# A decoder layer whose half-steps multiply weights in pairs by seven products: the plain groups in another order, one operand in two pieces, sums made tile by tile

## The chip, the core and the metric

The kernel runs on one core of a Trainium2 chip. Metric: device microseconds of one execution; 2087.26 us is the median of three runs before the change.

## What is computed

One layer on 256 tokens of width 2048: a SwiGLU half-step, a mixer (dilated attention beside gated linear attention), a cross-attention into 256 memory tokens, and a second SwiGLU half-step. The change lies in the half-steps alone:

```
def swiglu(h, w_gate, w_up, w_down):
    return (jax.nn.silu(h @ w_gate) * (h @ w_up)) @ w_down
x = x + 0.5 * swiglu(rms_norm(x, ffn1_norm[l]), ffn1_w_gate[l], ffn1_w_up[l], ffn1_w_down[l])
```

The inner width is 5632. Weights and activations are float32.

## The kernel before

**Products.** Every operand is split in two: a rounded part (`wh`, by a ScalarE cast) and a remainder (`wl`, by a VectorE subtraction), both at line 189. A product of a 128-row block is three matmuls: rounded by rounded, rounded by remainder, remainder by rounded.

**Tiles.** The 5632 inner columns are 11 tiles of 512, worked in three parts of 4, 4 and 3 tiles (`PARTS`). For each tile, gate and up are multiplied with the 16 row blocks of x. Behind a part's tiles come two steps of the down projection, each for two of the four output chunks. The two half-steps do the same, the first at 0 to 780 us of the span and the second from 1290 on.

**The pair step** (`strassen`, line 279). Gate and up of one tile, or two chunks of down, are taken together; left and right below. Tile 0's gate and up are multiplied plainly (they also make the sums of x), so a half-step has 16 pair steps: 10 for tiles 1 to 10, 6 for down. Ten of the 16 row blocks (sets a and b of `SEVEN`, five each) go through seven products instead of eight, for both halves of the tokens:

- 1: a's left block; 2: a's left plus right; 3: that plus b's right; 4: b's left; 5: a's right plus b's right; 6: b's right; 7: the sum of product 3 plus b's left.
- Products 2, 3, 5 and 6 multiply sums of token halves (`sh`, `sl`), which are made beforehand: of x once for a half-step, of the inner tiles once for each part.
- The sums of 2 and 3 are made on VectorE (`add`, line 295) in the buffer of a's left block, so the second add waits until the remainder of product 2 has been read out of it. The sums of 5 and 7 are made by accumulating DMAs from GpSimd's queue (`accumulate`, line 301).

The other six row blocks go plainly (`whole`, line 232), in a long group of four and a short group of two (`PLAIN`); each group is a left and a right block. Order before: products 1 to 6, long left, product 7, long right, short left, short right.

**What sets the order.** Loads are issued by SP in program order, casts and remainders in the same order (`in_turn`). Five raw places go round (`places`); a load waits until the old content of its place has been read, by the accumulate too. `wh` and `wl` have three buffers each (`FWB`), so the cast of an operand waits until TensorE is done with the operand three places ahead. A scheduler then sets each engine's order by priority; each engine works strictly in its order.

**The inner tile.** Behind the step, Silu on ScalarE and one VectorE product for each token half give `h`. `turn` (line 457), due two products later, transposes it (eight small matmuls `tp`), splits it into `hTh` and `hTl` from PSUM. The part's token sums (`sums_of`, line 246) are written behind product 6 of the part's last tile: `hTh` and `hTl` are added again, combined by four VectorE operations, and split. The sums of x are stored to DRAM after tile 1 (line 518) and read back behind a part's second down step (line 492), since both use the same buffers. In the first half-step, x is copied into an accumulation buffer in DRAM (line 521), onto which half the down outputs are added (line 538).

Of the kernel before, what the change touches and what calls it, by code (L numbers as in the profile page):

```python
# [8 lines left out]
F32 = mybir.dt.float32  # L9
# [3 lines left out]
ALU = mybir.AluOpType  # L13
# [3 lines left out]
P = 128  # L17
S = 256
TT = S // P
D = 2048  # L20
NC = D // 512
# [33 lines left out]
def layer_kernel(ctx: ExitStack, tc: tile.TileContext, A: dict, out: bass.AP):  # L55
# [68 lines left out]
    def later(n, fn):  # L124
        pend.append([n, fn])
# [62 lines left out]
    def split(wh, wl, src):  # L188
        return SC.copy(wh, src), V.tensor_sub(wl, src, wh.bitcast(F32))  # L189
# [50 lines left out]

    def new_sums():
        return tuple(FT(n, 1, [P, 2, WK, S], F32R, n) for n in ("sh", "sl"))

    def sums_of(ga, gb, more=None):


        t0, t1 = slice(0, P), slice(P, S)
        sums = new_sums()  # L250
        fs = [[CT([P, 4, S], F32, n) for n in ("fa", "fb")]]
        for f, (h, l) in zip(fs[0], (ga, gb)):
            V.tensor_add(f, h.bitcast(F32), l.bitcast(F32))
        if more:
            f5 = W2([P, 2, S], "f5")
            V.tensor_add(f5, *(x.bitcast(F32) for x in more))
            fs.append([f5[:, i:i + 1] for i in range(2)])
        for fa, fb in fs:
            V.tensor_sub(fb[:, :, t1], fa[:, :, t1], fb[:, :, t1])
            V.tensor_sub(fa[:, :, t1], fa[:, :, t0], fa[:, :, t1])  # L260
            V.tensor_sub(fa[:, :, t0], fb[:, :, t1], fa[:, :, t0])
            V.tensor_add(fb[:, :, t0], fb[:, :, t0], fa[:, :, t0])
        for i, f in enumerate(fs[0]):
            split(*(x[:, i, :4] for x in sums), f)
        if more:
            split(*(x[:, :, 4] for x in sums), f5)
        return sums

    def product(acc, lhs, w, start):

# [8 lines left out]
    def strassen(Wl, cl, Wr, cr, lhs, ab, sums, groups, mid=None, last=False):  # L279

        a, b = ab
        (ral, pal), (rar, par) = load(Wl, cl, a), load(Wr, cr, a)
        (rbr, pbr), (rbl, pbl) = load(Wr, cr, b), load(Wl, cl, b)
        places.extend((pbl, par, pbr))

        def parts(src):
            m = len(a)
            with tc.high_priority(WPRI):
                wh, wl = (wtile(x, m) for x in ("wh", "wl"))
                wsplit(wh, wl, src)  # L290
            return [(wh[:, i], wl[:, i]) for i in range(m)]

        def add(dst, x, y):
            with tc.high_priority(WPRI):
                V.tensor_add(dst, x, y)  # L295

        def accumulate(dst, x):
            with tc.high_priority(WPRI):
                for ks in (slice(0, 4), slice(4, len(a))):
                    if ks.start < len(a):  # L300
                        G.dma_start(dst[:, ks], x[:, ks], accum_op=ALU.add)  # L301
# [71 lines left out]
    def split_from_psum(hi, lo, ps):  # L373
        SC.copy(hi, ps)
        V.tensor_sub(lo, ps, hi.bitcast(F32))
# [76 lines left out]
    def ffn(pre, r, after, fine=None, last=False):  # L452

        wg, wu, wd = (A[f"{pre}_w_{n}"] for n in ("gate", "up", "down"))
        hT = {}

        def turn(f, hs, own):
            hi, lo = (FT("h", 6, [P, 4, S], F32R, n) if own < 3 else CT([P, 4, S], F32R, n) for n in ("hTh", "hTl"))
            for t in range(TT):
                tp = PM([P, 4, P], "tp")  # L460
                for j in range(4):
                    PE.transpose(tp[:, j], hs[t][:, j * P:(j + 1) * P], ident)
# [10 lines left out]
        for part in PARTS:  # L473
# [2 lines left out]

            g = [list(group(f)) for f in part]
            if len(part) == 4:
                seven, plain = (g[0] + g[2][:1], g[1] + g[2][1:2]), (g[3], g[2][2:])
            else:  # L480
                seven, plain = g[:2], g[2:]

            def sums_h():
                more = [x[:, 0:2] for x in hT[part[2]]] if len(part) == 4 else None
# [9 lines left out]
            for i, f in enumerate(part):  # L494
                if sums is None:
                    gate, upv = plain_pair(wg, f, wu, f, lhs_x, range(NC), fine)
                    with tc.high_priority(120):
                        sums = sums_of(xT[2], xT[3], [x[:, 2:4] for x in xT[1]])
                    if callable(r):
                        r = r()  # L500
                else:
                    gate, upv = strassen(wg, f, wu, f, lhs_x, SEVEN, sums, PLAIN,
                                         mid=sums_h if f == part[-1] else None)
                sg, hs = [], []
                with tc.high_priority(WPRI):
                    for t in range(TT):
                        s = W2([P, 512], "sg")
                        SC.activation(s, gate[t], AF.Silu, scale=r[:, t:t + 1])
                        sg.append(s)
                    for t in range(TT):  # L510
                        h = W2([P, 512], "h")
                        V.scalar_tensor_tensor(h, upv[t], r[:, t:t + 1], sg[t], op0=ALU.mult, op1=ALU.mult)
                        hs.append(h)
                later(2, lambda f=f, hs=hs, i=i: turn(f, hs, i))
# [684 lines left out]
```

## Time and profile before

| | |
|---|---|
| median of 3 runs | 2087.26 us (2082.5 to 2090.44) |
| the profiled execution, by its time | 2083.18 us |
| its span | 2081.4 us |
| mean granted TensorE clock | 0.956 |
| TensorE / VectorE / ScalarE busy | 94% / 74% / 55% |
| DMA: bytes moved, mean rate | 490.67 MB, 236 GB/s |

Busy shares are of the span; TensorE's includes time at a lower granted clock. A row of the timeline gives start, duration, engine, line, tile and shape, and in brackets how long the engine had been idle and what ended that. A row of a stretch gives its length, busy time of PE, PEld, DVE, ACT and POOL with counts, the granted clock, the DMA engines' mean busy share and GB/s. PE is TensorE, DVE VectorE, ACT ScalarE, POOL GpSimd, SP the queue of the loads.

### The profile page before, as it was taken

The numbers are of one execution on the slowest core, as the hardware profiler recorded it, in microseconds if no ns is written. First come the engines' busy times: TensorE is split into PE (matmuls) and PEld (weight loads), VectorE is DVE, ScalarE is ACT, GpSimd is POOL, SyncE is SP. The second block draws the span as 40 slices with busy tenths as digits, with TensorE's granted clock in tenths as the row PEclk, the third lists the DMA queues.
The fourth block names the chain that finished last, engine by engine and source line by source line (L and its number), as shares of the span: only waits on it lengthen the run. The fifth ranks groups of instructions, "written<-read, shape, count | busy, mean of one in ns | idle before, by whom it ended". The sixth has DMA issues, their size and how long they took to land.

```text
span 2081.4 us, 22095 instructions
## 1 busy us (share of the span) xinstructions
PE 1955.1 (94%) x8532; PEld 1590.2 (76%) x8532; DVE 1535.1 (74%) x1179; ACT 1145.8 (55%) x1081; POOL 211.4 (10%) x243
## 2 busy tenths in 40 slices
PE   8999889999999999999999999999999999989998
PEld 6777777777777777878888888877777777767776
DVE  7788767788667896536785656888876788767786
ACT  6555555555555565644576455465555555555553
POOL 2001111000110010002220000000011000110000
PEclk9999999999999999999999999999999999998999
DMA  9877897777897776445465555767799776897776
GB/s 366 281 232 222 237 286 229 228 223 246 262 313 247 234 234 246 162 142 197 170 222 215 182 182 192 268 212 230 220 292 313 252 243 216 238 284 229 230 240 212
DMA packets 100022, 490.67 MB, mean 236 GB/s; under 512 B 11179, under 2 KB 12331, under 8 KB 53708
## 3 DMA queue, kind: packets, MB, share of 16 engines
q1 hardware_dynamic: 72556, 371.80, 47.3%
q0 software_dynamic: 26208, 115.36, 25.2%
q10 hardware_dynamic: 1152, 2.10, 0.3%
q8 instruction: 67, 1.10, 0.2%
q14 instruction: 39, 0.32, 0.0%
HBM read 388.54 MB, written 20.97 MB: 197 GB/s over the span
## 4 chain that ended last, share of the span: by engine, by line
PE 45%; DVE 9%; ACT 5%; DMA 1%; issue 1%; ACTq 0%; POOL 0%; POOLq 0%; SPq 0%
PE x L274 8%; PE acc L224 8%; PE acc L225 8%; PE acc L223 8%; ACT wh L189 5%; PE acc L274 5%; PE acc L232 5%; DVE wl L189 4%; DVE raw L295 4%; PE x L232 2%; DMA raw<-in_ffn_w_down_dram 1%; DMA raw<-raw 0%; DMA out_dram<-xc 0%; PE tp L415 0%; PE dsp L774 0%
## 5 line engine op out<-in xcount | busy, mean ns | idle before, releaser
L189 DVE TENSOR_TENSOR wl<-raw,wh 128x1024 fp32r<-128x1024 f32 (+3 forms) x538 | 1061.0, 1992 | 425.7 <-ACT wh L189 384.6
L189 ACT CAST wh<-raw 128x1024 fp32r<-128x1024 f32 (+3 forms) x538 | 884.5, 1664 | 653.2 <-PE acc L225 145.5
L223 PE MATMUL acc<-wh,xTh 128*128 128x512 f32 x544 | 215.0, 397 | 7.7 <-ACT wh L189 7.7
L224 PE MATMUL acc<-wl,xTh 128*128 128x512 f32 x544 | 214.4, 394 | 2.1 <-DVE wl L189 1.9
L225 PE MATMUL acc<-wh,xTl 128*128 128x512 f32 x544 | 213.5, 393 | 0.0
L274 PE MATMUL x<-wh,sh 128*128 128x512 f32 x312 | 111.8, 500 | 104.1 <-ACT wh L189 104.1
L301 POOL DMA_DIRECT2D raw<-raw x120 | 106.7, 1047 | 1001.0 <-DVE raw L295 632.7
L295 DVE TENSOR_TENSOR raw<-raw 128x2560 f32<-128x2560 f32 (+1 forms) x64 | 176.5, 2757 | 2.0
L274 PEld LDWEIGHTS x<-wh,sh 128*128 128x128 f32 x312 | 71.3, 240 | 127.4 <-ACT wh L189 113.4
L223 PEld LDWEIGHTS acc<-wh,xTh 128*128 128x128 f32 x544 | 102.3, 189 | 31.4 <-ACT wh L189 9.6
L224 PEld LDWEIGHTS acc<-wl,xTh 128*128 128x128 f32 x544 | 103.0, 189 | 26.7 <-DVE wl L189 5.8
L225 PEld LDWEIGHTS acc<-wh,xTl 128*128 128x128 f32 x544 | 103.0, 189 | 21.3
L274 PE MATMUL x<-wh,sl 128*128 128x512 f32 x312 | 107.5, 486 | 0.0
L232 PE MATMUL acc<-wh,xTl 128*128 128x512 f32 x360 | 94.6, 389 | 0.0
L232 PE MATMUL acc<-wl,xTh 128*128 128x512 f32 x360 | 94.6, 389 | 0.0
L232 PE MATMUL acc<-wh,xTh 128*128 128x512 f32 x360 | 94.6, 389 | 0.0
L274 PEld LDWEIGHTS x<-wh,sl 128*128 128x128 f32 x312 | 76.8, 246 | 19.6
L274 PE MATMUL x<-wl,sh 128*128 128x512 f32 x312 | 86.4, 408 | 0.3 <-DVE wl L189 0.3
L232 PEld LDWEIGHTS acc<-wh,xTl 128*128 128x128 f32 x360 | 67.6, 188 | 14.0
L232 PEld LDWEIGHTS acc<-wl,xTh 128*128 128x128 f32 x360 | 67.6, 188 | 14.0
L232 PEld LDWEIGHTS acc<-wh,xTh 128*128 128x128 f32 x360 | 67.6, 188 | 14.0
L274 PEld LDWEIGHTS x<-wl,sh 128*128 128x128 f32 x312 | 64.1, 206 | 16.1 <-DVE wl L189 0.7
(364 smaller groups left out, 2958.6 us busy)
## 6 DMA issues: line engine op xcount, KB each, us to landing
raw<-in_ffn_w_down_dram SPq DMA_DIRECT2D x72, 1024.0 KB, 7.3
raw<-in_ffn_w_up_dram SPq DMA_DIRECT2D x67, 1024.0 KB, 7.7
raw<-in_ffn_w_gate_dram SPq DMA_DIRECT2D x66, 1024.0 KB, 9.6
raw<-raw POOLq DMA_DIRECT2D x64, 1024.0 KB, 6.9
raw<-in_w_in_dram SPq DMA_DIRECT2D x48, 1024.0 KB, 4.8
raw<-in_w_out_dram SPq DMA_DIRECT2D x16, 1024.0 KB, 4.8
raw<-raw POOLq DMA_DIRECT2D x56, 256.0 KB, 7.7
raw<-in_ffn_w_gate_dram SPq DMA_DIRECT2D x44, 256.0 KB, 9.9
```

Of the source, the lines that this page charges most:

```text
L189: return SC.copy(wh, src), V.tensor_sub(wl, src, wh.bitcast(F32))
L223: PE.matmul(acc[t], lh, wh, start=first and i == 0, stop=False, skip_group_check=seeded)
L224: PE.matmul(acc[t], lh, wl, start=False, stop=False, skip_group_check=seeded)
L225: PE.matmul(acc[t], ll, wh, start=False, stop=last and i == len(half) - 1, skip_group_check=seeded)
L232: PE.matmul(acc[t], lhs(w[0], t)[i], w[1 + j], start=False, stop=last and j == 1 and n == len(group) - 1, skip_group_check=True)
L274: PE.matmul(acc, lhs(k)[i], w[k][j], start=first, stop=j == 1 and k == len(w) - 1, skip_group_check=not start)
L295: V.tensor_add(dst, x, y)
L301: G.dma_start(dst[:, ks], x[:, ks], accum_op=ALU.add)
```

## The change

1. `PLAIN` and the down projection's plain groups are turned round: short group first. Product 7 comes behind the first group's right block where there are two groups (the last part's down has one, and keeps its order).
2. The operand of product 2 is made in two pieces, of two row blocks and three: two adds, two casts, two remainders.
3. In `turn`, tiles 0 and 1 of a part, and in a part of four two blocks of tile 2, are also copied from PSUM to float32 by ScalarE, and combined there; only the split is left behind product 6.
4. The stores of the sums of x, and in the first half-step the copies of x into DRAM, are issued behind the last accumulate of tile 1's pair step.

```diff
-PLAIN = ((0, 1, 2, 3), (4, 5))
+PLAIN = ((4, 5), (0, 1, 2, 3))
...
-        def parts(src):
+        def parts(src, cut=()):
...
-                wsplit(wh, wl, src)
+                for i, j in zip((0,) + cut, cut + (m,)):
+                    wsplit(wh[:, i:j], wl[:, i:j], src[:, i:j])
...
-                V.tensor_add(dst, x, y)
+                for i, j in zip((0,) + cut, cut + (len(a),)):
+                    V.tensor_add(dst[:, i:j], x[:, i:j], y[:, i:j])
...
-                        G.dma_start(dst[:, ks], x[:, ks], accum_op=ALU.add)
+                        queued["sum"] = G.dma_start(dst[:, ks], x[:, ks], accum_op=ALU.add)
...
-        add(ral, ral, rar)
+        add(ral, ral, rar, (2,))
         accumulate(rar, rbr)
-        product(y, s_(0), parts(ral), True)
+        product(y, s_(0), parts(ral, (2,)), True)
...
-                if i == j == 0:
+                if i == 0 and j == min(len(groups) - 1, 1):
                     places.append(pal)
                     product(x, of(b, 1), parts(ral), False)
...
-        def turn(f, hs, own):
+        def turn(f, hs, own, fs):
+            if own < 2:
+                fs[own] = CT([P, 4, S], F32, "f")
+            elif own == 2 and len(fs) == 3:
+                fs[own] = W2([P, 2, S], "f5")
...
+                    if own < len(fs):
+                        SC.copy(fs[own][:, :, sl], tp[:, :fs[own].shape[1]])
+            if own == 1:
+                combine(*fs[:2])
+            elif own == 2 and len(fs) == 3:
+                combine(fs[2][:, 0:1], fs[2][:, 1:2])
...
-                seven, plain = (g[0] + g[2][:1], g[1] + g[2][1:2]), (g[3], g[2][2:])
+                seven, plain = (g[0] + g[2][:1], g[1] + g[2][1:2]), (g[2][2:], g[3])
...
-                    hsums.append(sums_of(hT[part[0]], hT[part[1]], more))
+                    hsums.append(split_sums(fs, fs[2] if len(fs) == 3 else None))
...
-                    for x, d in zip(sums, kept):
-                        G.dma_start(d, x.bitcast(F32))
-                    if fine:
-                        for c in range(NC):
+                    with tc.issue_after(queued["sum"].ins):
+                        for x, d in zip(sums, kept):
+                            G.dma_start(d, x.bitcast(F32))
+                        for c in range(NC) if fine else ():
```

What the scheduler makes of it. First TensorE in the first down step of the first half-step, behind product 6: `acc` and `x` at line 232 are the left and right plain blocks, with the matmul count behind the shape; `x` at line 274 (280 after) is product 7. Before:

```order
L232 MATMUL acc<-wh,hTh 128x512 x4
L232 MATMUL x<-wh,hTh 128x512 x4
L232 MATMUL acc<-wh,hTl 128x512 x4
L232 MATMUL x<-wh,hTl 128x512 x4
L232 MATMUL acc<-wl,hTh 128x512 x4
L232 MATMUL x<-wl,hTh 128x512 x4
L274 MATMUL x<-wh,hTh 128x512 x5
L274 MATMUL x<-wh,hTl 128x512 x5
L274 MATMUL x<-wl,hTh 128x512 x5
L232 MATMUL acc<-wh,hTh 128x512 x8
L232 MATMUL acc<-wh,hTl 128x512 x8
L232 MATMUL acc<-wl,hTh 128x512 x8
```

After:

```order
L232 MATMUL acc<-wh,hTh 128x512 x2
L232 MATMUL x<-wh,hTh 128x512 x2
L232 MATMUL acc<-wh,hTl 128x512 x2
L232 MATMUL x<-wh,hTl 128x512 x2
L232 MATMUL acc<-wl,hTh 128x512 x2
L232 MATMUL x<-wl,hTh 128x512 x2
L232 MATMUL acc<-wh,hTh 128x512 x4
L232 MATMUL acc<-wh,hTl 128x512 x4
L232 MATMUL acc<-wl,hTh 128x512 x4
L280 MATMUL x<-wh,hTh 128x512 x5
L280 MATMUL x<-wh,hTl 128x512 x5
L280 MATMUL x<-wl,hTh 128x512 x5
```

Both short blocks (12 matmuls each) now stand ahead of product 7, and behind it come both long blocks (24 each) instead of the right long and both short ones.

Second, TensorE in the second down step, from the end of product 4 on, after the change; `x` is product 5, `acc` with `sh` product 6:

```order
L280 MATMUL acc<-wl,hTh 128x512 x5
L232 MATMUL acc<-wh,hTh 128x512
L280 MATMUL x<-wh,sh 128x512 x5
L280 MATMUL x<-wh,sl 128x512 x5
L280 MATMUL x<-wl,sh 128x512 x5
L280 MATMUL acc<-wh,sh 128x512 x5
L280 MATMUL acc<-wh,sl 128x512 x5
L280 MATMUL acc<-wl,sh 128x512 x5
L232 MATMUL acc<-wh,hTh 128x512
```

Before, product 5 followed product 4 at once:

```order
L274 MATMUL acc<-wl,hTh 128x512 x5
L274 MATMUL x<-wh,sh 128x512 x5
L274 MATMUL x<-wh,sl 128x512 x5
L274 MATMUL x<-wl,sh 128x512 x5
L274 MATMUL acc<-wh,sh 128x512 x5
L274 MATMUL acc<-wh,sl 128x512 x5
L274 MATMUL acc<-wl,sh 128x512 x5
L232 MATMUL acc<-wh,hTh 128x512 x4
```

The first matmul of the short left block has moved ahead of product 5. That is so in 12 of the 32 pair steps.

Third, VectorE in the gate and up of the first half-step's tile 2, from the remainder of product 1. Before (line 295 is the add, 512 makes `h`, 375 is the remainder of a transposed tile, 253 the sums' add):

```order
L189 TENSOR_TENSOR wl<-raw,wh 128x2560
L295 TENSOR_TENSOR raw<-raw 128x2560
L512 SCALAR_TENSOR_TENSOR h<-acc,r_492,sg 128x512 x2
L189 TENSOR_TENSOR wl<-raw,wh 128x2560
L295 TENSOR_TENSOR raw<-raw 128x2560
L375 TENSOR_TENSOR hTl<-tp,hTh 128x4x128 x2
L253 TENSOR_TENSOR fb<-hTh,hTl 128x1024
L189 TENSOR_TENSOR wl<-raw,wh 128x2560 x2
```

After (the same are lines 303, 531 and 383):

```order
L189 TENSOR_TENSOR wl<-raw,wh 128x2560
L303 TENSOR_TENSOR raw<-raw 128x1024
L303 TENSOR_TENSOR raw<-raw 128x1536
L189 TENSOR_TENSOR wl<-raw,wh 128x1024
L189 TENSOR_TENSOR wl<-raw,wh 128x1536
L531 SCALAR_TENSOR_TENSOR h<-acc,r_492,sg 128x512
L303 TENSOR_TENSOR raw<-raw 128x2560
L531 SCALAR_TENSOR_TENSOR h<-acc,r_492,sg 128x512
L189 TENSOR_TENSOR wl<-raw,wh 128x2560 x2
L383 TENSOR_TENSOR hTl<-tp,hTh 128x4x128 x2
```

The first add and the second product's remainder are in two pieces, the product for `h` stands behind them, half of it behind the second add, and the sums' add is gone from this place.

More of the change, by code (lines that the diff above doesn't have):

```diff
@@ L235, in whole, with combine, split_sums, sums_of @@
                 tick()
+    queued = {}
     def new_sums():
         return tuple(FT(n, 1, [P, 2, WK, S], F32R, n) for n in ("sh", "sl"))
-    def sums_of(ga, gb, more=None):
+    def combine(fa, fb):
         t0, t1 = slice(0, P), slice(P, S)
-        sums = new_sums()
[L251 to L265, printed above, removed]
+        V.tensor_sub(fb[:, :, t1], fa[:, :, t1], fb[:, :, t1])
+        V.tensor_sub(fa[:, :, t1], fa[:, :, t0], fa[:, :, t1])
+        V.tensor_sub(fa[:, :, t0], fb[:, :, t1], fa[:, :, t0])
+        V.tensor_add(fb[:, :, t0], fb[:, :, t0], fa[:, :, t0])
+    def split_sums(f, f5):
+        sums = new_sums()
+        for i in range(2):
+            split(*(x[:, i, :4] for x in sums), f[i])
+        if f5 is not None:
             split(*(x[:, :, 4] for x in sums), f5)
         return sums
+    def sums_of(ga, gb, more):
+        f = [CT([P, 4, S], F32, n) for n in ("fa", "fb")]
+        f5 = W2([P, 2, S], "f5")
+        for x, (h, l) in zip(f + [f5], (ga, gb, more)):
+            V.tensor_add(x, h.bitcast(F32), l.bitcast(F32))
+        combine(*f)
+        combine(f5[:, 0:1], f5[:, 1:2])
+        return split_sums(f, f5)
     def product(acc, lhs, w, start):
@@ L289, in parts, with add @@
                 wh, wl = (wtile(x, m) for x in ("wh", "wl"))
-                wsplit(wh, wl, src)
+                for i, j in zip((0,) + cut, cut + (m,)):
+                    wsplit(wh[:, i:j], wl[:, i:j], src[:, i:j])
             return [(wh[:, i], wl[:, i]) for i in range(m)]
-        def add(dst, x, y):
+        def add(dst, x, y, cut=()):
             with tc.high_priority(WPRI):
-                V.tensor_add(dst, x, y)
+                for i, j in zip((0,) + cut, cut + (len(a),)):
+                    V.tensor_add(dst[:, i:j], x[:, i:j], y[:, i:j])
         def accumulate(dst, x):
@@ L478, in ffn @@
             if len(part) == 4:
-                seven, plain = (g[0] + g[2][:1], g[1] + g[2][1:2]), (g[3], g[2][2:])
+                seven, plain = (g[0] + g[2][:1], g[1] + g[2][1:2]), (g[2][2:], g[3])
             else:
                 seven, plain = g[:2], g[2:]
+            fs = [None] * (len(part) - 1)
             def sums_h():
-                more = [x[:, 0:2] for x in hT[part[2]]] if len(part) == 4 else None
                 with tc.high_priority(WPRI):
-                    hsums.append(sums_of(hT[part[0]], hT[part[1]], more))
+                    hsums.append(split_sums(fs, fs[2] if len(fs) == 3 else None))
             def sums_back():
```

2 lines of the change are left out of this document (1 added, 1 removed).

## The prediction

> **What bounds the kernel now.** I read the page first, then TensorE's waits, then three long stretches.
>
> ```profile
> span 2081.4 us, 22095 instructions
> PE 1955.1 (94%) x8532; PEld 1590.2 (76%) x8532; DVE 1535.1 (74%) x1179; ACT 1145.8 (55%) x1081; POOL 211.4 (10%) x243
> PE x L274 <- ACT wh L189: 104.1, 32, 3.9
> 57.00:780.00 723.00, 668.08 (x2790) 539.23 (x2789) 566.54 (x319) 397.32 (x276) 72.32 (x86) 0.94 0.80 247
> 780.00:1290.00 510.00, 508.89 (x2474) 424.30 (x2473) 314.38 (x443) 286.47 (x443) 49.90 (x46) 1.00 0.53 188
> 1340.00:2010.00 670.00, 621.67 (x2613) 502.78 (x2612) 524.73 (x292) 367.40 (x251) 67.45 (x79) 0.94 0.80 248
> ```
>
> TensorE carries the time. It loses most in one place: 32 times, once per pair step, product x (line 274) waits for a cast, 104.1 us in all. The stretches (length, then busy PE, PEld, DVE, ACT, POOL, granted clock, DMA share) show a second loss: in both half-steps the mean clock is 0.94, in the attention part between them 1.00 with PE busy 508.89 of 510, so dense work alone does not lower it. What does is the wait:
>
> ```profile
> 406.00:408.00 2.00, 2.00 (x6) 1.52 (x6) 2.00 (x1) 2.00 (x2) 0.00 (x0) 0.50 0.01 4
> 736.96 1.21 PE L274 MATMUL x<-wh,sh 128*128 128x512 f32 x4 [2.08 <-ACT wh L189]
> ```
>
> Right behind a wait of 3.4 us the clock is 0.50; behind one of 2.08 us four matmuls take their usual time. Now one step in order of time (start, duration, idle before and what ended it), the end of one pair step and the start of the next:
>
> ```profile
> 434.66 2.34 ACT L189 CAST wh<-raw 128x2560 fp32r<-128x2560 f32 x1 [3.70 <-PE acc L232]
> 437.03 2.82 DVE L189 TENSOR_TENSOR wl<-raw,wh 128x2560 fp32r<-128x2560 f32 x1 [4.11 <-ACT wh L189]
> 439.89 2.83 DVE L295 TENSOR_TENSOR raw<-raw 128x2560 f32<-128x2560 f32 x1
> 441.71 1.30 PE L274 MATMUL x<-wh,xTh 128*128 128x512 f32 x5
> 442.63 1.40 DVE L512 SCALAR_TENSOR_TENSOR h<-acc,r,sg 128x512 f32<-128x512 f32 x2
> 442.81 2.34 ACT L189 CAST wh<-raw 128x2560 fp32r<-128x2560 f32 x1 [2.80 <-DVE raw L295]
> 445.18 2.83 DVE L189 TENSOR_TENSOR wl<-raw,wh 128x2560 fp32r<-128x2560 f32 x1 [1.14 <-ACT wh L189]
> 448.04 2.83 DVE L295 TENSOR_TENSOR raw<-raw 128x2560 f32<-128x2560 f32 x1
> 449.33 0.60 PE L462 MATMUL tp<-ident,h 128*128 128x128 f32 x4
> 450.95 4.55 ACT L189 CAST wh<-raw 128x2560 fp32r<-128x2560 f32 x2 [0.35 <-DVE raw L295]
> 453.33 2.07 PE L274 MATMUL x<-wh,sh 128*128 128x512 f32 x4 [3.40 <-ACT wh L189]
> ```
>
> This is a serial chain of 18.67 us: cast of product 1, its remainder, first add, cast of product 2, its remainder, second add, cast of product 3 (453.33 - 434.66). Its first cast has idled 3.70 us and starts when TensorE frees a `wh` buffer, 7.05 us before product 1 starts (441.71). So it ends 11.6 us after that start, while products 1 and 2 and the transposes occupy TensorE for less than 8.
>
> **The change part by part.** The prices, first of a matmul (fifteen in 3.40 us, sixteen in 3.64: 0.2275 us each), then of the pieces:
>
> ```profile
> 1376.00 3.40 PE x L274 x15
> 1379.40 3.64 PE acc L232 x16
> L189 DVE TENSOR_TENSOR wl<-raw,wh 128x2560 fp32r<-128x2560 f32 x196 | 548.5, 2822 | 191.3 <-ACT wh L189 191.2
> L189 DVE TENSOR_TENSOR wl<-raw,wh 128x1024 fp32r<-128x1024 f32 x246 | 302.8, 1242 | 191.8 <-ACT wh L189 150.9 <-PE x L274 32.6 <-PE x L232 7.6
> L189 ACT CAST wh<-raw 128x2560 fp32r<-128x2560 f32 x196 | 451.8, 2334 | 238.3 <-PE acc L232 96.3 <-DVE raw L295 75.2 <-PE x L274 33.0
> L189 ACT CAST wh<-raw 128x1024 fp32r<-128x1024 f32 x246 | 256.2, 1052 | 275.8 <-PE acc L225 145.5 <-PE x L274 78.2 <-PE x L232 31.4
> L374 ACT CAST hTh<-tp 128x512 fp32r<-128x512 f32 x44 | 26.0, 590 | 45.3 <-PE tp L462 45.3
> L512 DVE SCALAR_TENSOR_TENSOR h<-acc,r,sg 128x512 f32<-128x512 f32 x44 | 31.1, 744 | 2.0 <-PE acc L225 1.5 <-PE acc L232 0.5
> L253 DVE TENSOR_TENSOR fa<-hTh,hTl 128x1024 f32<-128x1024 f32 x6 | 7.3, 1224 | 0.2
> ```
>
> *Short blocks first.* Three `wh` buffers go round, so product 1's cast takes the buffer of the operand three places ahead. Now that is the right long block; behind its last use come 8 + 24 matmuls, 7.3 us by the price, 7.05 seen. With the long blocks last it is the seventh product's; behind that come 5 + 48 matmuls, 12.1 us, less the same 0.25: 11.8.
>
> *Second operand in two pieces.* From the two sizes, a piece of 1536 costs 1.77 us on VectorE and a cut 0.17. The first piece's cast now runs beside the second add, and the second piece's beside the first remainder, so add, cast, remainder shrink from 2.83 + 2.34 + 2.83 = 8.0 to two adds and two remainders, 3.01 + 3.01 = 6.0: 2.0 us a step. [...]
>
> The new chain: 2.34 + 2.83 + 3.01 + 3.01 + 0.74 (one h now stands ahead of the second add) + 2.83 + 2.34 + 0.3 of gaps = 17.4 us; the Silu that now stands ahead of the second cast waits for the gate's last matmul, 24 matmuls or 5.5 us ahead of product 1, and adds up to 0.9. It ends 5.6 to 6.5 us after product 1's start. TensorE wants it after 30 matmuls, 6.8 us, or with a tile's eight transposes (2 x 0.60, overlapping) about 7.8. The wait at product 3 goes, and with it the half clock.
>
> *Sums in steps.* A part of four tiles loses two adds of 1.22 us and one of half that on VectorE and gains four copies of 0.59 and two smaller ones on ScalarE, busy 55%. Zero, covered by ScalarE's idle time; if the cover fails, 3 us in each of six parts.
>
> The ceiling from the stretches: idle 723 - 668.08 = 54.9 and 670 - 621.67 = 48.3; lost clock 0.06 x 723 = 43.4 and 0.06 x 670 = 40.2; together 186.8. About 4 of it stays: a half-step's first pair step has no pair step ahead, and its last follows the one-group order, which is as it was. That leaves 182.8, or 6.5 for each of 28 steps.
>
> What is late next:
>
> ```profile
> 408.63 1.75 POOL L301 DMA_DIRECT2D raw<-raw  x2 [11.44 <-DVE wl L189]
> 416.90 0.33 SPq L179 DMA_DIRECT2D raw<-in_ffn_w_up_dram  x1
> 421.73 1.92 ACT L189 CAST wh<-raw 128x2048 fp32r<-128x2048 f32 x1 [1.73 <-DMA raw<-in_ffn_w_up_dram]
> 214.48:262.18 47.70, 43.55 (x178) 34.91 (x178) 33.26 (x16) 25.30 (x18) 7.06 (x8) 0.93 0.87 250
> 262.18:309.94 47.76, 43.64 (x177) 34.95 (x177) 33.30 (x16) 25.41 (x18) 8.19 (x10) 0.93 0.92 295
> 309.94:357.71 47.77, 44.36 (x185) 35.94 (x186) 37.03 (x21) 25.58 (x18) 3.49 (x4) 0.93 0.82 248
> 405.53:453.33 47.80, 44.40 (x185) 35.93 (x185) 39.53 (x26) 25.59 (x18) 3.49 (x4) 0.93 0.74 231
> sl<-ffn_sl POOLq DMA_DIRECT2D x4, 1280.0 KB, 9.9
> sh<-ffn_sh POOLq DMA_DIRECT2D x4, 1280.0 KB, 13.4
> raw<-in_ffn_w_up_dram SPq DMA_DIRECT2D x22, 512.0 KB, 6.5
> ```
>
> The DMA share, times the length, is 35.4 us in a plain gate/up step and 41.5 + 43.9 + 39.2 = 124.6 in the three that hold down work; TensorE needs some 41 for each (177 matmuls, 40.3, and transposes). So the engines fit in the first and are full in the three.
>
> - Behind a part's second down step the kept sums are read back (2 x 1280 KB) beside the loads. If the two queues share, the next step's first operand comes about 6 us late and its wait stays: 4 x 7 = 28 us. If loads went first it would be 0. The landings (9.9, 13.4) are those of sharing, so I take 28. [...]
> - `issue_after` puts the stores of the kept sums, in the first half-step the copies of x too, behind the last accumulate of tile 1, where the next step's loads start: twice 0 to 6, taken as 12. Later accumulates queue behind them on GpSimd, SP's loads share the engines with them. The copies of x leave the start of the program; I take 0 for that, since no row here prices it alone.
> - In 12 steps (the last gate/up step of the four parts of four tiles, their second down, and the step after it) one matmul of the left short block stands ahead of product 5. It waits for ScalarE, which from product 3 on must do four casts, two copies and the short cast, 4 x 2.33 + 2 x 0.58 + 1.05 = 11.6 us, from 3 us after product 1's start: 14.6, where TensorE is there at 13.6. 1.0 in eight steps, 2.4 in the four with the copies of the sums besides: 18.
> - Full DMA engines in the second down: 4 x 2 = 8. Remainders of the sums ahead of a part's first down, the size of two adds of 1.22 and one of half that, half hidden: 4 x 1.5 = 6. Combining tiles 0 and 1 on VectorE, four operations of half a 1024 (0.71 each by the two sizes), half hidden: 6 x 1.4 = 8.
>
> Together 80. Several fall on the same steps, where one wait covers another; I take three quarters, 60 (bounds 0 and 110). So 182.8 - 60 = 122.8 gained. The profiled execution took 2083.18 us by its time (span 2081.4), 4.1 below the median 2087.26 of the runs: 1960.4 on its scale, **1964 us** as a median.
>
> **The rivals.**
>
> *Nearly all of it* (leftovers under 30): for it, the margins above and loads that land 4.8 us after issue (416.90 to 421.73); against it, the full engines in the downs. At zero leftovers 2087.3 - 182.8 = 1904.
>
> *Only the pieces count*: first operands land too late for the earlier cast in most steps, and the chain is only 2.0 us shorter: 28 x 2.0 = 56, 2031. For it, the DMA share: 35.4 of 41 us is 0.86 against 0.74. Against it, the first cast's idle time was ended by TensorE, not by a DMA.
>
> *The right short block's load, slower.* It goes into the place whose old content the second accumulate reads, so it cannot start before that has landed. TensorE reaches the block four products and 12 matmuls behind product 3's start, 72 x 0.2275 = 16.4 us; the right long block, which had that place, came 6.1 us later (8.9 behind product 6 instead of 2.7). From product 3's cast: remainder 2.82, accumulate 408.63 to 416.90 and a start of 0.3, 8.6, load 4.8, cast 1.05: 17.3, less the cast's lead of about 1.2, so 16.1. It fits by 0.3. A wait over 3.4 us also costs some 3.0 of half clock. It is slower than before when wait and clock exceed 6.5, a wait of 3.5 and more: when in nearly every step the load lands 8.6 us after issue or later, not 4.8 (the row of 512 KB has 6.5 as its median). At 11 us: wait 5.9 + 3.0 = 8.9, 2.4 x 28 = 67 slower, 2154.
>
> *No difference*: that wait lies between 2 and 3.4 and the downs lose as much as the gate/up steps gain, about 2085.
>
> **How the numbers follow.** 0.5% (10.4 us) is what a measurement of this kernel can tell. Forecast, leftovers 30 to 110 (1934 to 2014): 0.56. Nearly all: 0.17. Only the pieces: 0.17. No difference: 0.04. Slower: 0.06. The range goes from 1908, short of the ceiling, to 2045, past the pieces alone; about 0.2 lies outside. Faster 0.56 + 0.17 + 0.17 = 0.90, same 0.04, slower 0.06.
>
> **What would show it.** Right: the wait of x (line 280 then) for a cast falls from 104 to under 30 us, product 1's cast starts about 12 us ahead of its first matmul, plain gate/up steps last 41 to 42.5 us, the clock in the half-steps is above 0.97, and what waits remain stand behind second downs and at the matmul ahead of product 5. Wrong: the cast of the right short block waits for its DMA with TensorE behind it, or the cast of product 1 does; or steps keep 45 us and more.

## The result and the profile after

1995.28 us in the median of four runs (1993.42 to 1996.78), against 2084.88 of the kernel before in four runs; the ratio is 0.957, its 95% interval 0.9541 to 0.9598. The profiled execution took 1996.78 us, its span 1994.7. That is faster, as forecast and inside the range, but 31 us above the forecast of 1964: of the 122.8 us forecast, 86.7 came by the spans of the two profiled executions (2081.4 - 1994.7; 89.6 by the medians). The question of the study is where the other 36 went.

The page's span and busy shares, TensorE's list of waits, and three stretches that hold the same work as the three shown of before:

```profile
span 1994.7 us, 22276 instructions
PE 1908.7 (96%) x8532; PEld 1553.2 (78%) x8532; DVE 1519.0 (76%) x1227; ACT 1149.3 (58%) x1145; POOL 209.5 (11%) x243
...
PE x L280 <- ACT acc L322: 26.9, 19, 4.3
PE acc L232 <- ACT wh L189: 25.6, 13, 5.3
...
PE x L280 <- ACT wh L189: 4.2, 1, 4.2
...
50.00:736.80 686.80, 644.74 (x2793) 519.60 (x2792) 561.51 (x344) 400.38 (x311) 75.46 (x91) 0.98 0.85 265
736.80:1246.60 509.80, 509.41 (x2477) 424.95 (x2476) 312.97 (x442) 286.17 (x442) 50.33 (x47) 1.00 0.52 187
1296.40:1931.50 635.10, 604.91 (x2623) 488.20 (x2622) 518.15 (x315) 371.48 (x284) 68.19 (x81) 0.98 0.85 265
```

The wait of product x for a cast, 104.1 us before, is 31.1 now (26.9 + 4.2; line 322 is the copy of product 1's sum, which stands behind product 3's cast), just above the 30 that the forecast named as a sign. A new wait of 25.6 us has come at the plain blocks (line 232). The clock in the half-steps is 0.98 against 0.94; the middle stretch is as it was. The next rows are the same chain as before, in a plain gate/up step:

```profile
367.77 2.35 ACT L189 CAST wh<-raw 128x2560 fp32r<-128x2560 f32 x1 [1.46 <-DVE wl L189]
370.16 2.83 DVE L189 TENSOR_TENSOR wl<-raw,wh 128x2560 fp32r<-128x2560 f32 x1 [0.20 <-ACT wh L189]
373.02 2.90 DVE L303 TENSOR_TENSOR raw<-raw 128x1024 f32<-128x1024 f32 x2
374.33 1.05 ACT L189 CAST wh<-raw 128x1024 fp32r<-128x1024 f32 x1 [2.04 <-DVE raw L303]
375.95 1.48 ACT L189 CAST wh<-raw 128x1536 fp32r<-128x1536 f32 x1
377.75 1.30 PE L280 MATMUL x<-wh,xTh 128*128 128x512 f32 x5
379.80 2.82 DVE L303 TENSOR_TENSOR raw<-raw 128x2560 f32<-128x2560 f32 x1
382.73 2.34 ACT L189 CAST wh<-raw 128x2560 fp32r<-128x2560 f32 x1 [5.30 <-DVE raw L303]
385.61 1.40 PE L280 MATMUL x<-wh,sh 128*128 128x512 f32 x5
```

The chain lasts 17.3 us (382.73 + 2.34 - 367.77), its first cast starts 10.0 us ahead of product 1, and product 3 follows at once, with no idle time in brackets. Four steps as stretches, each from one product y to the next (plain; with the copies of the sums; behind a read-back; behind the stores):

```profile
338.40:381.10 42.70, 42.12 (x186) 33.70 (x186) 36.20 (x22) 25.99 (x20) 3.48 (x4) 1.00 0.82 260
423.60:469.80 46.20, 43.44 (x187) 35.13 (x187) 40.45 (x30) 28.21 (x23) 3.48 (x4) 0.96 0.79 242
290.30:338.40 48.10, 42.45 (x178) 33.97 (x177) 37.91 (x22) 26.88 (x20) 7.88 (x9) 0.96 0.96 283
57.30:112.90 55.60, 45.34 (x187) 36.43 (x186) 36.78 (x21) 27.80 (x21) 9.38 (x12) 0.91 0.86 287
```

A plain step is within 0.2 us of what was forecast (41 to 42.5), and TensorE is busy for 42.12 of its 42.70. The three others are the leftovers: one costs 3 to 5 us, one 7, one 14.

### The profile page after: what moved, and what is told of

It reads as the page before. It is cut to its first block, busy times and chain, and to the rows that moved or that the text cites. A ratio compares the mean times of both kernels' runs of the same rounds, so it can differ in the third digit from the quotient of the medians.

```text
span 1994.7 us, 22276 instructions
## 1 busy us (share of the span) xinstructions
PE 1908.7 (96%) x8532; PEld 1553.2 (78%) x8532; DVE 1519.0 (76%) x1227; ACT 1149.3 (58%) x1145; POOL 209.5 (11%) x243
## 4 chain that ended last, share of the span: by engine, by line
PE 41%; DVE 9%; DMA 7%; issue 6%; ACT 4%; POOL 0%; SPq 0%; ACTq 0%; DVEq 0%; POOLq 0%
PE acc L224 8%; PE acc L225 8%; PE acc L223 8%; DVE wl L189 6%; PE x L280 5%; DMA raw<-in_ffn_w_gate_dram 5%; PE acc L232 4%; ACT wh L189 3%; PE acc L280 2%; DMA raw<-raw 2%; DVE raw L303 2%; PE x L232 1%; PE y L280 1%; DMA raw<-in_ffn_w_down_dram 1%; DMA raw<-in_ffn_w_up_dram 0%
## 5 line engine op out<-in xcount | busy, mean ns | idle before, releaser
L189 DVE TENSOR_TENSOR wl<-raw,wh 128x1024 fp32r<-128x1024 f32 (+4 forms) x570 | 1062.7, 1885 | 383.3 <-ACT wh L189 380.8
L189 ACT CAST wh<-raw 128x1024 fp32r<-128x1024 f32 (+4 forms) x570 | 890.1, 1584 | 659.9 <-DVE raw L303 193.3
L303 DVE TENSOR_TENSOR raw<-raw 128x1024 f32<-128x1024 f32 (+3 forms) x96 | 178.6, 1887 | 1.3
L280 PE MATMUL x<-wh,sh 128*128 128x512 f32 x312 | 94.8, 436 | 36.2 <-ACT acc L322 26.9
L280 PEld LDWEIGHTS x<-wh,sh 128*128 128x128 f32 x312 | 59.9, 204 | 56.8 <-ACT acc L322 33.4
L232 PEld LDWEIGHTS acc<-wh,xTh 128*128 128x128 f32 x360 | 67.6, 190 | 38.5 <-ACT wh L189 24.9
L280 PE MATMUL x<-wh,sl 128*128 128x512 f32 x312 | 88.5, 416 | 0.0
L232 PEld LDWEIGHTS acc<-wl,xTh 128*128 128x128 f32 x360 | 68.4, 190 | 14.5
L280 PEld LDWEIGHTS x<-wl,sh 128*128 128x128 f32 x312 | 58.3, 195 | 22.6 <-DVE wl L189 10.9
L280 PEld LDWEIGHTS x<-wh,sl 128*128 128x128 f32 x312 | 63.9, 205 | 15.2
```

What stands on the lines that cost most here:

```text
L232: PE.matmul(acc[t], lhs(w[0], t)[i], w[1 + j], start=False, stop=last and j == 1 and n == len(group) - 1, skip_group_check=True)
L280: PE.matmul(acc, lhs(k)[i], w[k][j], start=first, stop=j == 1 and k == len(w) - 1, skip_group_check=not start)
L303: V.tensor_add(dst[:, i:j], x[:, i:j], y[:, i:j])
```

## The experiments

The theory: order and pieces shorten the chain's delay together, and what is left are separate costs (read-back, stores, a matmul ahead of its turn) that add up. The rival: one of the two parts does it all, and the leftovers cover one another, as the forecast assumed.

**Order alone** (the kernel before, with the short groups first and product 7 behind both short blocks):

```
-PLAIN = ((0, 1, 2, 3), (4, 5))
+PLAIN = ((4, 5), (0, 1, 2, 3))
...
```

> The kernel before with the plain groups and product 7 in the new order, nothing else. Theory (the lead of product 1's cast is what counts): the chain of 18.7 us, with both products for h ahead of the second add 20.1, now starts 11.8 us before product 1 and ends 6.9 to 8.3 us after its start; the wait of x for a cast falls from 104 us to 10 to 45, the half clock behind it goes, 1995 to 2020 us. Rival (the two pieces carry the gain): the wait stays above 70 us, 2050 us or more.

2041.60 us, ratio 0.9788 (0.9772 to 0.9804): 43 us gained, between the two expectations. The wait of x for a cast is 72.4 us, where 10 to 45 or above 70 was expected.

**Pieces alone** (the kernel before, product 2's operand in two pieces):

```
...
-        product(y, s_(0), parts(ral), True)
+        product(y, s_(0), parts(ral, (2,)), True)
```

> The kernel before with the operand of product 2 in two pieces, nothing else. As the prediction priced it (2.0 us for each of 28 steps): 2030 us. Rival (the wait need only fall below some 2 us, since the half clock behind it, about 3 us a step, then goes too): the wait falls from 3.4 to about 1.4 us, 5 us saved in most steps, 1940 to 1975 us.

2032.83 us, ratio 0.9750 (0.9735 to 0.9765): 52 us. That is the time expected at the prediction's price, but not by the way expected, as the rows below show; neither part alone is the whole cause. With the order alone the first cast starts earlier, but is now ended by a DMA, and product 3 still waits:

```profile
372.93 2.35 ACT L189 CAST wh<-raw 128x2560 fp32r<-128x2560 f32 x1 [1.71 <-DMA raw<-in_ffn_w_gate_dram]
382.72 1.29 PE L274 MATMUL x<-wh,xTh 128*128 128x512 f32 x5
392.80 1.43 PE L274 MATMUL x<-wh,sh 128*128 128x512 f32 x5 [2.23 <-ACT wh L189]
```

With the pieces alone, timeline, then stretches of the same step:

```profile
418.88 2.34 ACT L189 CAST wh<-raw 128x2560 fp32r<-128x2560 f32 x1 [3.71 <-PE acc L232]
425.93 1.30 PE L274 MATMUL x<-wh,xTh 128*128 128x512 f32 x5
426.92 1.40 DVE L514 SCALAR_TENSOR_TENSOR h<-acc,r,sg 128x512 f32<-128x512 f32 x2
436.78 1.42 PE L274 MATMUL x<-wh,sh 128*128 128x512 f32 x5 [3.00 <-ACT wh L189]
...
433.78:436.78 3.00, 0.00 (x1) 0.01 (x1) 2.80 (x7) 3.00 (x4) 0.00 (x0) 1.00 0.49 87
436.78:438.20 1.42, 1.42 (x6) 1.21 (x7) 1.42 (x2) 1.42 (x1) 0.00 (x0) 1.00 0.00 0
438.20:441.60 3.40, 3.40 (x9) 2.66 (x9) 3.40 (x2) 3.40 (x3) 1.54 (x2) 0.50 0.14 29
```

The lead is 7.05 us as before (425.93 - 418.88). The chain is only 0.8 us shorter (436.78 - 418.88 = 17.90 for 18.67), since both `h` (1.40 us) now stand ahead of the second product's remainder. The wait falls by 0.4, from 3.40 to 3.00. The rest comes from the clock: it is 0.50 for 3.40 us here, and for 6.78 in the kernel before (below), of which 1.05 lie in the wait itself, so TensorE loses 1.2 us less ((5.73 - 3.40) / 2).

That is one step; the clock does not do the same behind every wait of 3.00 us (last section). The sum over the 28 steps that the forecast counts, each from one product y to the next, fourteen in a half-step, is worked out from the traces: idle is the time without a matmul, lost clock the missing part of the granted clock while there is one.

| 28 steps, us | length | TensorE idle | clock lost at work |
|---|---|---|---|
| before | 1324.1 | 99.0 | 70.1 |
| order alone | 1279.9 | 87.8 | 32.5 |
| pieces alone | 1281.0 | 89.1 | 42.6 |
| order and pieces | 1240.4 | 63.6 | 12.2 |
| the changed kernel | 1250.8 | 67.6 | 20.9 |

Each part alone takes some 10 us of idle time and about three times that in clock: with the pieces, a small cut of the wait took two fifths of the clock's loss with it.

**Order and pieces**, sums and stores as in the kernel before:

> The kernel before with the new order and the two pieces, but with the sums of the inner tiles made as before and the stores of x's sums and copies of x where they were. If the later stores cost the changed kernel its long step behind tile 1 (55.6 us) and give back 7 us at the start, this is 5 to 15 us faster than the changed kernel: 1980 to 1990 us. Rival (the sums in steps save time): 2000 to 2010 us.

1991.65 us, ratio 0.9552 (0.9538 to 0.9566). 42.8 and 51.6 us alone make 94.4; together they give 92.8 (2084.41 - 1991.65). The two add up, and they are the whole gain: sums in steps and later stores together give nothing (3.6 us lost, with intervals that overlap). The time lies between the two expectations.

**No pieces** (the changed kernel, product 2's operand whole):

> The changed kernel with the operand of product 2 in one piece. Theory (lead): product 3's cast is 2.0 us later and comes 0 to 1 us after TensorE wants it; the matmul of the short block ahead of product 5 is gone from this order too, which gives back some 4 us in each of 4 to 8 steps: 1985 to 2005 us. Rival (pieces carry it): 2040 us or more.

2056.15 us, ratio 0.9858 (0.9842 to 0.9875): beside all the rest, the pieces are worth 61 us. The theory's 1985 to 2005 missed, the rival's 2040 or more came. It is also 14.5 us slower than the order alone (2041.60), so without the pieces the sums in steps and the later stores together lose time; why is open.

**Stores where they stood before** (the changed kernel without `issue_after`):

```
-                    with tc.issue_after(queued["sum"].ins):
-                        for x, d in zip(sums, kept):
-                            G.dma_start(d, x.bitcast(F32))
+                    for x, d in zip(sums, kept):
+                        G.dma_start(d, x.bitcast(F32))
...
```

> The changed kernel without one part: the stores of the kept sums and the copies of x stand where they stood before, ahead of the first tile's sums, instead of behind its first accumulate. If those stores, landing behind the first accumulate, are what makes the second step of each first tile long (55.6 and 47.4 us from one product y to the next), these two steps come down to some 48 and 43, a gain of about 11 us, while the first product y of the kernel comes later (57.3 us now, 64.3 in the kernel before), a loss of up to 7: 1985 to 1993 us. If the long steps come from the sums made in steps and not from the stores, both steps stay and only the start is lost: about 2002 us.

1987.12 us, ratio 0.9533 (0.9516 to 0.9549). The two first steps fall from 55.6 and 47.4 to 48.8 and 41.7 us, and the first product y comes at 63.1 instead of 57.3. So the later stores cost 6.8 and 5.7 us in these steps and won 5.8 at the start; moving them was no gain (8.2 us lost by the medians, with intervals that just touch). In the first half-step 7.5 us over the 41.3 of a step without losses stay even so.

**No read-back:**

```
-                        G.dma_start(x.bitcast(F32), d)
+                        G.memset(x.bitcast(F32), 0.5)
```

> The changed kernel with the kept sums not read back: the two tiles are filled with a constant by GpSimd instead, so the 2.5 MB of read-back behind each second down step is left out and the products with the sums work on a constant. If the read-back holds up the loads, the four steps behind a second down (48.2, 48.9, 49.4 and 48.1 us) come down to the 42.3 of the plain steps, and their waits of 4.3 us with them: some 25 us less, 1970 us. If the wait there comes from the second down step itself (the order of its casts) and the read-back is only carried alongside, the steps stay above 46 and the time within 8 us: 1987 us or more.

1972.55 us, ratio 0.9461 (0.9445 to 0.9478). The four steps of 48.2, 48.9, 49.4 and 48.1 us become 44.4, 42.2, 42.5 and 43.9. First the changed kernel, behind the first read-back, then the same place without it:

```profile
282.40 2.34 ACT L189 CAST wh<-raw 128x2560 fp32r<-128x2560 f32 x1 [5.92 <-DMA raw<-in_ffn_w_gate_dram]
286.88 1.30 PE L280 MATMUL x<-wh,xTh 128*128 128x512 f32 x5
299.64 2.50 PE L280 MATMUL x<-wh,sh 128*128 128x512 f32 x5 [4.27 <-ACT acc L322]
```

```profile
276.28 2.35 ACT L189 CAST wh<-raw 128x2560 fp32r<-128x2560 f32 x1 [1.62 <-DMA raw<-in_ffn_w_gate_dram]
286.75 1.30 PE L280 MATMUL x<-wh,xTh 128*128 128x512 f32 x5
293.55 1.43 PE L280 MATMUL x<-wh,sh 128*128 128x512 f32 x5
```

The first cast's lead goes from 4.5 to 10.5 us: the 6 us by which the forecast let the first operand be late.

**No matmul ahead of its turn:**

```
...
+                    behind(mm, ran["product"])
...
```

(each plain matmul is held behind the last matmul of the product written ahead of it, without a semaphore)

> The changed kernel with one rule more for the scheduler: no matmul of a plain group is issued ahead of the last product of its pair. In the changed kernel a lone matmul of the plain group goes ahead of product 5 in eight places and waits 2.45 to 2.49 us there in four of them, with the clock at 0.50 behind. If that lone matmul, waiting at the head of TensorE's queue for a cast that comes later, is the cost, the four steps of 46.1 us come down to 42.3 and the second downs lose their waits of 1.0 to 1.7: some 15 to 20 us less, 1975 to 1980 us. If TensorE is held there by the loads and would wait anyway, a wait of the same size appears at the first matmul of product 5 or of the plain group, and the time stays at 1990 to 1996 us.

1998.62 us, ratio 0.9587 (0.9568 to 0.9606): no difference. The lone matmul, which the forecast had as the one that waits, is not the cost; as the second expectation said, a wait of the same size appears at product 5. First the changed kernel, then this one:

```profile
166.15 4.59 ACT L189 CAST wh<-raw 128x2560 fp32r<-128x2560 f32 x2
170.63 0.66 ACT L479 COPY f<-tp 128x256 f32<-128x256 f32 x2
171.15 0.62 ACT L328 COPY ys<-y 128x512 f32<-128x512 f32 x1
172.00 0.69 DVE L332 TENSOR_TENSOR acc<-ys,x 128x512 f32<-128x512 f32 x1
172.77 0.73 PE L232 MATMUL acc<-wh,xTh 128*128 128x512 f32 x1 [2.46 <-ACT wh L189]
```

```profile
172.90 0.61 ACT L335 COPY ys<-y 128x512 f32<-128x512 f32 x1
173.75 0.69 DVE L339 TENSOR_TENSOR acc<-ys,x 128x512 f32<-128x512 f32 x1
174.50 1.42 PE L287 MATMUL x<-wh,sh 128*128 128x512 f32 x5 [2.48 <-DVE acc L339]
```

The real wait is one place on. Product 5 writes over `x`, so it needs the subtraction that reads x (line 332); that needs the copy of y (line 328), and this copy stands on ScalarE behind two casts (4.59 us) and the new copies of the sums (line 479). Here three of those steps last 44.5 us instead of 46.1, as no half clock follows the wait, and one 45.8, where it does (last section); but product 5 waits 0.6 to 2.0 in the second downs and behind them. The kernel with order and pieces alone, which has no copies of the sums, has no wait at product 5 in these four steps, but one of 1.7 us at product 3.

**The copy ahead of product 3's cast** (line 322, ordered ahead on ScalarE):

```
...
+                    if copy is not None:
+                        behind(cast, copy)
...
```

> The changed kernel with the copy of product 1's sum (line 322) held ahead of the cast of product 3 on ScalarE. The waits list puts 26.9 us in 19 places at product 3 down to this copy of 0.57 us, which stands behind that cast. If the copy's place is the cost, each of these waits falls by the copy and the time by about 0.5 x 28 = 14 us: 1981 us. If the cast is what came late and the copy is only the last of the two to end, the waits stay, now named for the cast, less the 0.5 us at most where product 3 sets the step: 1987 to 1997 us.

2000.72 us, ratio 0.9586 (0.9571 to 0.9601), the same as the changed kernel's within the intervals, 4 us past the second expectation. In the four steps behind a read-back product 3 waits 3.8 us instead of 4.3, the copy's half a microsecond less, and now for the cast: there the row that named the copy named the last to finish, not the cause. Elsewhere the order on the engines changed too: x waits 47.3 us for a cast in all, 2.2 to 2.8 of it in each of the four first down steps, and the plain blocks wait 15.0 instead of 25.6. So the equal time doesn't price the copy by itself.

**Places handed on in another order** (the next right short block goes into the place that the first accumulate frees):

```
-        places.extend((pbl, par, pbr))
+        places.extend((par, pbl, pbr))
```

> The changed kernel with the two freed places of a pair handed on in the other order, so that the next loads of the right short block go into the place that the first, not the second, accumulate frees. If a plain step is now bound by a loop (remainder of product 3, second accumulate of 8.4 us, loads of about 13 us, chain of 17.3 us, remainder 2.8: 42 us), the loop is opened, the waits of 1.6 and 4.3 us at product 3 go down and the plain steps fall from 42.3 to the 41.2 us of TensorE's own work: some 20 us less, 1975 us, more if the plain group's lone matmuls go too. If the lead of product 1's cast is set by when its own load may start (the buffers of the long blocks) and not by this accumulate, the plain steps stay at 42.2 to 42.7 us and the time within 4 us: 1992 to 1999 us.

1969.66 us, ratio 0.9441 (0.9422 to 0.9461): near the time expected, for the most part for another reason. Of the 23.2 us by which the 28 steps are shorter, 12.5 come from the four steps of 46.1 us, now 42.5, 43.1, 42.7 and 43.6. The eight plain steps (from tiles 5, 6, 9 and 10 of each half-step) fall by 5.6 together, 0.7 each where 1.1 was expected. With the places the scheduler's order has changed: no plain matmul stands ahead of product 5 any more, and on ScalarE one cast stands ahead of the copies, not two:

```profile
164.98 2.37 ACT L189 CAST wh<-raw 128x2560 fp32r<-128x2560 f32 x1
167.22 0.68 ACT L479 COPY f<-tp 128x256 f32<-128x256 f32 x2
167.74 0.65 ACT L328 COPY ys<-y 128x512 f32<-128x512 f32 x1
170.00 1.31 PE L280 MATMUL x<-wh,sh 128*128 128x512 f32 x5
```

Product 5 starts without a wait. So the loop through the second accumulate, on which that expectation rested, isn't shown, and can hold no more than the smaller part.

**Stores, read-back and places at once:**

> Three of the single edits at once on the changed kernel: the stores and the copies of x where they stood before, the sums not read back (the two tiles are filled with a constant, so the read-back is left out), and the freed places handed on in the other order. Alone they took 8.2, 22.7 and 25.6 us from the changed kernel's 1995.3, 56.5 us in sum. If the leftovers of the changed kernel lie on different steps and simply add up, the time is 1995.3 - 56.5 = 1939 us (within 4). If they overlap, as the prediction took them when it counted three quarters of their sum, it is 1995.3 - 42 = 1953 us.

1932.16 us, ratio 0.9253 (0.9235 to 0.9271). Singly they gave 8.2 + 22.7 + 25.6 = 56.5; together 63.1. The surplus of 6.6 is within the noise of the changed kernel's own time (ratio 0.9541 to 0.9598), but a quarter less, 42, is not: these leftovers do not cover one another. The others of the forecast's list (full engines in the downs, remainders, combining) were not taken away singly.

**Stores and places, everything computed:**

> The stores and the copies of x where they stood before, and the freed places handed on in the other order, with everything computed. If the two add up: 1995.3 - 8.2 - 25.6 = 1961.5 us, the fastest complete kernel of the study. If they overlap to a quarter: 1970 us, no better than the other order of the places alone (1969.7).

1956.67 us, ratio 0.9373 (0.9358 to 0.9388), the fastest kernel here that computes everything, 38.6 us under the changed one, where 33.8 was the sum of the two.

**The same with product 7 behind the left short block:**

> As the kernel with stores, copies and places, and the seventh product behind the left short block instead of behind both. The right short block's load gets the 3.4 us of the seventh product as cover. If that load is still waited for in the steps of the read-back and in the first tiles (48 to 52 us each), these come down by up to 3 us each: 1950 to 1958 us. If the first product's load, issued when the left short block's subtraction is done, is what a step now turns around, nothing that stands behind that subtraction helps, and the time is within 4 us of the kernel with stores, copies and places.

1959.53 us, ratio 0.9385 (0.9361 to 0.9410): no difference, so more cover for the right short block's load buys nothing. What holds the plain steps at 42 us, and not at the 41.0 that a few of them reach, stays open; of the changed kernel's plain step above, 0.58 us is idle time of TensorE (42.70 - 42.12).

## Why the prediction held, point by point

**The ceiling was counted twice in part.** 182.8 us took idle time and lost clock as separate. One wait of the kernel before, cut where the clock changes:

```profile
449.93:452.28 2.35, 0.00 (x0) 0.00 (x0) 2.31 (x4) 2.00 (x3) 0.00 (x0) 1.00 0.47 85
452.28:453.33 1.05, 0.00 (x0) 0.00 (x0) 0.98 (x3) 1.05 (x2) 0.00 (x0) 0.50 0.00 0
453.33:459.06 5.73, 5.73 (x14) 4.47 (x15) 5.58 (x3) 5.47 (x3) 1.75 (x2) 0.50 0.22 46
```

The clock falls 1.05 us before the wait ends, while TensorE does nothing: 0.52 us of this step are in both numbers. Over the 28 steps the traces have 99.0 us idle and 83.6 of lost clock, 182.6 in sum, as forecast, but 13.5 of that clock was lost in the waits themselves. Measured by the steps: they last 666.8 + 657.3 = 1324.1 us before. At 47.8 - 6.5 = 41.3 us, the forecast's step without losses, they would be 1156.4, so 167.7 could be had, not 182.8.

**The lead of product 1's cast** was to be 11.8 us; it is 10.0. The buffer is free in time, but the operand isn't there, as in this other plain step of the changed kernel (product 1 follows at 335.05, 9.5 us later):

```profile
325.57 2.34 ACT L189 CAST wh<-raw 128x2560 fp32r<-128x2560 f32 x1 [2.67 <-DMA raw<-in_ffn_w_gate_dram]
...
335.05 1.30 PE L280 MATMUL x<-wh,xTh 128*128 128x512 f32 x5
```

That is the forecast's own sign for wrong (the cast of product 1 waits for its DMA), but the loss of 2 us was within what the chain could bear: 17.3 us as forecast (17.4), so it ends 7.3 us after product 1's start, where TensorE wants it after 6.8 to 7.8. The price of a cut was a little off: by the two sizes it is 0.19 us (1.77 + 1.24 - 2.82), not 0.17, and two adds end 2.90 us after the first starts (373.02), not 3.01.

**The leftovers** are the step that failed: 80 in sum, "I take three quarters, 60". Over 41.3 us a step, the 28 steps of the changed kernel (630.2 + 620.5 = 1250.7 us) lose 94.3:

| | forecast | measured |
|---|---|---|
| four steps behind the read-back | 28 | 29.4 |
| two first steps, behind the stores | 12 | 20.4 |
| four steps with the copies of the sums | 9.6 | 19.2 |
| eight down steps, ten other steps | 30 | 25.3 |

The read-back's price was right, and the stores' came out above the 0 to 6 a step given: behind them the right short block's cast waited for its DMA and TensorE for the cast, with the clock at 0.50 in the last 2.92 us of that wait and for 3.88 after it:

```profile
89.42 3.27 ACT L189 CAST wh<-raw 128x1024 fp32r<-128x1024 f32 x2 [13.73 <-DMA raw<-in_ffn_w_up_dram]
90.52 2.07 PE L232 MATMUL acc<-wh,xTh 128*128 128x512 f32 x4 [5.27 <-ACT wh L189]
```

In the steps with the copies, the wait's size was right (2.4; 2.46 measured), but the half clock behind it (a mean of 0.96 over the step of 46.20 us above) was left out, and without the lone matmul product 5 waits as long for the copy of y. The discount had no ground: the costs lie in different steps or at different points of one, and three taken away together gave no less than the three singly. The 80 should have stood whole, and was itself 14 short.

**Outside these steps** 13.3 us were gained that the forecast had at zero: the first product y comes at 57.3 us instead of 64.3, as the copies of x have left the start (the experiment with the stores takes 5.8 of it back), and from product y of the last pair step but one to the end it is 67.4 instead of 73.7. There the order is the old one, but the pieces count, which the forecast overlooked (70.1 with the pieces alone, 75.0 with the order alone).

So 167.7 - 94.3 + 13.3 = 86.7, where 182.8 - 60 was forecast: 15 too much ceiling, 34 too few leftovers, 13 not counted.

**Sums in steps**, priced at zero: order and pieces without them is 1991.65, the changed kernel without the later stores 1987.12, ratios 0.9552 and 0.9533 with intervals that overlap. But that is two effects that nearly cancel, not none: between these two kernels the four first down steps fall from 180.6 to 169.8 us together (product 3's wait of 2.6 us is all but gone there), and the four steps with the copies rise from 178.3 to 182.7. ScalarE had the idle time, but not at that place.

**The rivals.** *Only the pieces* gave 2031; the pieces alone measure 2032.83, but by a wait 0.4 shorter and half the clock's loss, not by a chain 2.0 shorter, so that number was right by luck, and the order adds 41 to it. *The right short block's load*: issued at 354.92 in the plain step shown, its cast starts at 359.40, 4.5 us later, and the block's first matmul at 360.51, as the cast ends and without a wait. It fits by a hair, as worked out; only behind the stores does it not (waits of 5.27 and 3.78 us). *Nearly all of it* failed by the read-back, the stores and the copies.

## What to carry to other kernels

Two losses at one place, a wait and the clock behind it, are added only after cutting the stretch where the clock changes (13.5 us were in both here); and separate leftovers are summed whole, unless one can say which wait covers which. Of a wait, look at what the waiting instruction writes over as well as at what it reads, and at everything ahead of the releaser on its engine, since the named releaser can be no more than the last to finish (with the copy ahead, the wait of 4.3 us at product 3 was still 3.8). What a wait costs in clock is counted over many waits, not read from one: of 22 of 3.00 to 3.05 us, 7 cost none. A new copy on an engine with idle time is not free where something that TensorE needs stands behind it (with the copies on ScalarE, busy 58%, four steps rose from 178.3 to 182.7 us).

## What the runs showed of the hardware

The clock fell in pieces of one length: 0.50 for 3.40 us after the wait of 3.00 shown with the pieces alone, for 6.78, twice that, after the wait of 3.40 in the kernel before. It fell while TensorE was idle (452.28, before) and 1.4 us after it had begun again (438.20, the pieces alone). The clock records in the traces give a piece as 3.413 us, and the falls lie on a grid of it: in the trace of the kernel before all 30 falls to 0.50 start a whole number of 3.413 us apart (within 0.01), and so they do in those of the pieces alone and of the changed kernel.

What followed a wait went with where it fell on this grid. With the pieces alone there are 22 waits of 3.00 to 3.05 us at product 3: 7 brought no half clock, 10 one piece and 5 two. The 7 start 0.43 to 0.61 of a piece behind a point of the grid, the 5 start 0.32 to 0.34 behind one, the 10 elsewhere. One of the 7:

```profile
163.27 1.42 PE L274 MATMUL x<-wh,sh 128*128 128x512 f32 x5 [3.00 <-ACT wh L189]
163.27:170.10 6.83, 6.83 (x30) 5.47 (x31) 6.83 (x5) 6.83 (x4) 1.75 (x2) 1.00 0.38 77
```

In the kernel before, 23 of 27 waits of 3.38 to 3.85 us brought two pieces. Its steps had settled at 47.8 us, which is 14 pieces (47.79), so that nearly each wait met the grid at the same, costly place; that the half clock itself kept them there is not shown. The forecast's 3.4 us was no bound: a wait of 3.40 in the kernel before (at 1494.86) brought no half clock, while waits of 3.00 did, and so did 2.46, in the changed kernel with one lone matmul behind the wait (a mean of 0.52 from 172.77 to 176.30), and in the one with no matmul ahead of its turn with five behind it:

```profile
1678.50 2.50 PE L287 MATMUL x<-wh,sh 128*128 128x512 f32 x5 [2.46 <-DVE acc L339]
1678.50:1681.40 2.90, 2.90 (x7) 2.32 (x8) 2.90 (x2) 0.00 (x0) 0.00 (x0) 0.50 0.26 47
```

The same wait at 174.50 of that kernel (2.48) brought none.
